# Three transformer layers on one core: one norm chain for both token tiles, and a reordered first and second layer

## The chip, the core and the metric

The kernel runs on one core of a Trainium2 chip. The metric is the device time of one execution in microseconds (us). The kernel before took 1570.29 us, the median of three runs (1568.15 to 1570.87).

## What is computed

256 tokens of width 1024 (two tiles of 128 tokens) pass through three layers, all in float32. Each layer normalises x by its root mean square, modulates it by vectors made from a condition c, mixes tokens, adds the result to x, normalises again and sends every token to two of its experts.

```python
def first_block(x, c, ...):                 # layers 0 and 1
    silu_c = jax.nn.silu(c)
    for i in range(DEPTH):
        mod = silu_c @ ada_w[i] + ada_b[i]
        sh1, sc1, g1, sh2, sc2, g2 = [m[:, None, :] for m in jnp.split(mod, 6, axis=-1)]
        h = rms_norm(x, norm_mix_g[i]) * (1.0 + sc1) + sh1
        y = diff_attention(h, ...) if i % N_MIXERS == 0 else chunked_attention(h, ...)
        x = x + g1 * y
        h = rms_norm(x, norm_ffn_g[i]) * (1.0 + sc2) + sh2
        x = x + g2 * grouped_moe(h, router_w, router_bias, moe_w_gate[i], moe_w_up[i], moe_w_down[i])
    return x

def rms_norm(x, g):
    y = xf * lax.rsqrt(jnp.mean(xf * xf, axis=-1, keepdims=True) + NORM_EPS)
    return (y * g.astype(jnp.float32)).astype(x.dtype)

def grouped_moe(h, router_w, ...):          # 16 experts in 4 groups: best group, top 2 inside it
    scores = jax.nn.sigmoid((t @ router_w).astype(jnp.float32))
    ...
    for e in range(N_EXPERTS):
        he = jax.nn.silu(t @ w_gate[e]) * (t @ w_up[e])
        out = out + gates[:, e:e + 1] * (he @ w_down[e])
```

Layer 2 is a hybrid: a small gated MLP over chunks, attention over the tokens and over 256 context tokens (`ctx`, normalised and modulated with vectors of their own), a gated scan in both directions, and then 32 experts in 4 groups of 8.

## The kernel before

**Stages.** The layers run one behind the other. Times of the profiled execution, from the start of the span: start to 55, layer 0's mixing to 176, its router 176 to 205, the gather of tokens 205 to 218, its experts 222 to 441; layer 1's mixing 455 to 600, router 602 to 633, gather 634 to 644, experts 646 to 893; layer 2's mixing 907 to 1087, experts 1104 to 1564.

**Weights.** Every weight tile of 1 MB is fetched by SyncE's queue (SP) into one of 17 buffers called `u`, in the order in which the program uses them; the normalised x takes one as well. An issue waits until the buffer that it gets is free. Dense weights are split into a rounded part and a remainder for exact float32 products: ScalarE casts 128x2048 elements (L185) and VectorE subtracts (L196). The products themselves are L265.

**Order.** Two strings, MIX_ORDER[0] and [1], list the steps of the layers 0 and 1 in program order, a letter a step; a scheduler then orders the instructions of each engine, starting from that. Letters that matter here: `0` the norm and its transposes; `J` the broadcast of a gate; `A` and `f` one tile of modulation products (`ada_tile`, L410); `5`-`8` scores and softmax of a pair of heads; `V` a projection of values; `W`-`Z` transposes and value products of a pair of heads (`a_trans` L636, `head1` L691 and L693); `9` one step of the context's preparation for layer 2; `M` the router of one token tile (transposes L499, logits L1385 to L1405); `U` the broadcast of the second gate (bias sum L417, L440 on TensorE); `E` the ranks of the tokens in their experts (L1524 to L1530); `L` the gather of the tokens (L1559); `!` the overflow loop (L1720, L1721), at which every engine waits for the others and SP's stream of weights stops; `u` one weight tile of the experts ahead.

**The norm.** `norm` (L450) calls `norm_tile` for each token tile: a square with row sums on ScalarE (L457), ten tiny VectorE operations for 1/rms (L283 to L299, a bit trick and three Newton steps), and the scaling on VectorE (L459). It is used where a layer begins and for the context; `trans_split` (L477) then transposes the result on TensorE, eight blocks a tile, and L514 (ScalarE) and L516 (VectorE) apply the modulation. The router calls `norm_tile` itself.

**The next layer's modulation.** `done(key)` computes the tiles of modulation products that are left and closes the sum (`ada_close`: copy out of PSUM, L417, the turn to columns L425). `layer` calls it for the next layer ahead of the experts (`body`). The experts go in pairs; `body` loads 12 weight tiles a pair, forms gate and up products (L1641), transposes (L1657), down products (L1670), and adds the weighted results to x (L1705, L1711), two at a time.

## Time and profile before

| | |
|---|---|
| median of three runs | 1570.29 us (1568.15 to 1570.87) |
| the profiled execution | 1569.43 us |
| its span in the profile | 1567.7 us |
| TensorE (PE) busy | 1434.1 us, 91% of the span |
| VectorE (DVE) busy | 630.1 us, 40% |
| ScalarE (ACT) busy | 405.4 us, 26% |
| GpSimd (POOL) busy | 111.7 us, 7% |
| transferred | 540.87 MB, mean 345 GB/s |

The profile is one execution on the chip. About 1.7 us of it lie around the span. Busy shares are means over stages with different limits, so they do not tell what a change in one stage is worth; the timeline of each engine in a stage, with what ended each wait, does. TensorE's granted clock (PEclk) has two levels: 1.00 stands for 2.4 GHz and 0.50 for 1.2 GHz.

### The profile page before, as it was taken

The numbers are of one execution on the slowest core, as the hardware profiler recorded it, in microseconds if no ns is written. First come the engines' busy times: TensorE is split into PE (matmuls) and PEld (weight loads), VectorE is DVE, ScalarE is ACT, GpSimd is POOL, SyncE is SP. The second block draws the span as 40 slices with busy tenths as digits, with TensorE's granted clock in tenths as the row PEclk, the third lists the DMA queues.
The fourth block names the chain that finished last, engine by engine and source line by source line (L and its number), as shares of the span: only waits on it lengthen the run. The fifth ranks groups of instructions, "written<-read, shape, count | busy, mean of one in ns | idle before, by whom it ended". The sixth has DMA issues, their size and how long they took to land. (4 is left out here: it accounts for less than half of the span.)

```text
span 1567.7 us, 18587 instructions
## 1 busy us (share of the span) xinstructions
PE 1434.1 (91%) x7202; PEld 763.8 (49%) x7202; DVE 630.1 (40%) x1434; ACT 405.4 (26%) x717; POOL 111.7 (7%) x96
## 2 busy tenths in 40 slices
PE   5999989999989989899999899688999999989987
PEld 1676643454346556444544375465445445434432
DVE  3777521221276675242221368966122212212112
ACT  2455211011053553142110256532111111011000
POOL 0000101101000001001000000101000101001000
PEclk8999879999999999999999999899999999999999
DMA  9987859999989948499999768238799999999997
GB/s 362 321 330 273 333 203 422 420 422 421 413 310 380 334 161 321 189 416 416 417 420 419 268 212 301 89 103 327 294 421 422 421 421 420 422 421 421 421 421 294
DMA packets 131072, 540.87 MB, mean 345 GB/s; under 512 B 8600, under 2 KB 13856, under 8 KB 83360
## 3 DMA queue, kind: packets, MB, share of 16 engines
q1 hardware_dynamic: 128032, 533.73, 85.9%
q10 hardware_dynamic: 2320, 3.89, 0.8%
q0 software_dynamic: 624, 1.98, 0.4%
q8 instruction: 60, 0.98, 0.3%
q14 instruction: 36, 0.29, 0.1%
HBM read 538.49 MB, written 1.06 MB: 344 GB/s over the span
## 5 line engine op out<-in xcount | busy, mean ns | idle before, releaser
L1641 PE MATMUL ps<-u,b 128*64 128x512 f32 x2048 | 486.2, 599 | 13.7 <-DMA u<-in_w_dram 9.7
L1641 PEld LDWEIGHTS ps<-u,b 128*64 128x64 f32 x2048 | 165.9, 138 | 302.0 <-issue 278.6
L265 PE MATMUL ps<-u 128*128 128x512 f32 x1104 | 278.6, 403 | 6.3 <-ACT u L514 5.1
L265 PEld LDWEIGHTS ps<-u 128*128 128x128 f32 x1104 | 203.7, 190 | 78.5 <-issue 21.6
L1670 PE MATMUL ps<-u,b 128*64 128x512 f32 x1024 | 232.5, 597 | 5.0 <-ACT b L1659 2.4
L1711 DVE TENSOR_TENSOR x<-x,ps 128x512 f32<-128x512 f32 x128 | 79.7, 682 | 209.6 <-PE ps L1705 209.6
L1670 PEld LDWEIGHTS ps<-u,b 128*64 128x64 f32 x1024 | 83.1, 136 | 126.2 <-issue 115.5
L1677 POOL TENSOR_TENSOR b<-b,b 128x512 fp32r<-128x512 f32 x58 | 78.1, 1362 | 808.9 <-ACT b L1676 713.1
L1675 DVE SCALAR_TENSOR_TENSOR b<-ps,tiny,G 128x512 f32<-128x512 f32 x64 | 48.1, 751 | 183.9 <-PE ps L1670 175.5
L1648 DVE TENSOR_TENSOR b<-b,ps 128x512 f32<-128x512 f32 x32 | 22.0, 688 | 224.5 <-PE ps L1641 132.3
L196 DVE TENSOR_TENSOR u<-u 128x2048 fp32r<-128x2048 f32 (+1 forms) x48 | 105.4, 2208 | 4.8 <-ACT u L185 4.6
L410 PE MATMUL ps<-u,z 128*32 128x512 f32 x576 | 85.4, 650 | 16.8 <-DVE z L379 13.1
L1676 ACT CAST b<-b 128x512 fp32r<-128x512 f32 x64 | 39.4, 618 | 208.7 <-DVE b L1675 208.7
L1659 ACT COPY b<-ps 128x512 f32<-128x512 f32 x32 | 18.8, 586 | 274.2 <-PE ps L1657 274.2
L185 ACT CAST u<-u 128x2048 fp32r<-128x2048 f32 x44 | 82.7, 1912 | 17.9 <-DMA u<-in_a_w_qkv_dram 15.3
L1559 PE MATMUL ps<-b,u 128*128 128x512 f32 x256 | 77.0, 447 | 3.1 <-DVE b L1545 3.1
L1559 PEld LDWEIGHTS ps<-b,u 128*128 128x128 f32 x256 | 66.7, 329 | 19.6 <-issue 13.5
L1705 PE MATMUL ps<-b,b 128*128 128x512 f32 x256 | 70.2, 410 | 3.3 <-DVE b L1677 1.9
L1646 ACT ACTIVATE b<-ps 128x512 f32<-128x512 f32 x32 | 19.1, 597 | 191.7 <-PE ps L1641 191.7
L1705 PEld LDWEIGHTS ps<-b,b 128*128 128x128 f32 x256 | 45.2, 188 | 41.8 <-ACT b L1646 16.2
L514 ACT ACTIVATE b<-ps,mod,mA 128x512 f32<-128x512 f32 x32 | 24.9, 779 | 109.4 <-PE ps L1559 109.4
L516 DVE TENSOR_SCALAR b<-ps,mA,mod 128x512 f32<-128x512 f32 x32 | 25.9, 810 | 66.3 <-PE ps L1559 66.3
(346 smaller groups left out, 1167.0 us busy)
## 6 DMA issues: line engine op xcount, KB each, us to landing
u<-in_w_dram SPq DMA_DIRECT2D x192, 1024.0 KB, 19.8
u<-in_moe_w_gate_dram SPq DMA_DIRECT2D x64, 1024.0 KB, 11.1
u<-in_moe_w_up_dram SPq DMA_DIRECT2D x64, 1024.0 KB, 12.6
u<-in_moe_w_down_dram SPq DMA_DIRECT2D x64, 1024.0 KB, 13.2
u<-in_ada_w_dram SPq DMA_DIRECT2D x48, 1024.0 KB, 10.3
u<-in_w_mod_dram SPq DMA_DIRECT2D x24, 1024.0 KB, 7.3
u<-in_w_in_dram SPq DMA_DIRECT2D x14, 1024.0 KB, 5.7
u<-in_a_w_qkv_dram SPq DMA_DIRECT2D x12, 1024.0 KB, 14.7
```

Source lines behind the costliest of these rows:

```text
L185: (e.copy if e is self.nc.scalar else e.tensor_copy)(out, in_)
L196: self.pick(site, options).tensor_tensor(out, a, b, op=op)
L265: self.nc.tensor.matmul(p, x[a][:, k, t * 128:(t + 1) * 128], w[b][:, k % 4], start=start and i == 0 and k == ks[0], stop=stop and i == 2 ...
L410: self.nc.tensor.matmul(st["R"][32 * j:32 * j + 32, :], z[:, k, 11 - i:43 - i], w[:, k, :], start=(n == 0 and k < 4), stop=(last and k >= ...
L1559: nc.tensor.matmul(p, q[:, t, k:D:KC], P[:, t], start=(t == 0 and i == 0), stop=(t == 1 and i == 1))
L1641: nc.tensor.matmul(p[s * 64:(s + 1) * 64, :], hs[k // 2][:, k % 2, c0 + s * 64:c0 + (s + 1) * 64], W[e0, nm, k // 4, s][:, k % 4, :], star ...
L1670: nc.tensor.matmul(po[n][s * 64:(s + 1) * 64, :], heT[:, k, s * 64:(s + 1) * 64], w(s), start=(k == 0), stop=(k == 3), skip_group_check=True)
L1675: V.scalar_tensor_tensor(o, po[n], gs, g2[:, n * 512:(n + 1) * 512], op0=OP.mult, op1=OP.mult)
L1676: A.copy(oh[:, n], o)
L1677: (G if more else V).tensor_tensor(ol[:, n], o, oh[:, n].bitcast(F32), op=OP.subtract)
L1705: ins = nc.tensor.matmul(p, PT[:, t * 128:(t + 1) * 128], o[:, n, :], start=(i == 0), stop=(i == len(ops) - 1))
L1711: nc.vector.tensor_add(xs, xs, p)
```

## The change

It has six parts.

- `norm` squares half rows: four ScalarE operations of 128x512, first the left halves of both tiles, then the right ones. The sums of both tiles go through **one** chain of operations on 128x2, which has 13 steps, since the shorter form of the Newton step needs a value of its own for each row. Tile 0 is scaled on VectorE and tile 1 on ScalarE.
- In the routers of the layers 0 and 1 a Sigmoid of a constant is computed after the second tile's copy; its result is not used.
- MIX_ORDER[0]: the last two `A` steps move from the stretch behind the gather to places around the ranks and the gate's broadcast. The closing of the next layer's modulation (`done`) moves from ahead of `body` to behind the down products of its first pair of experts.
- MIX_ORDER[1], softmax: the step `X` moves behind the first `8`.
- MIX_ORDER[1], router: `U` moves from between the two `M` to behind `E`, next to the ranks.
- `head1`: the products of two heads take turns, key tile by key tile, where one head came behind the other.

```diff
--- before.py
+++ after.py
@@ -121,8 +121,8 @@
 RAW = 2
 
...
-MIX_ORDER = ("00kkfkqiqvtfvqr4vf421321Kxw3xuzwzfKfyQKQyfVnTVQRAn55667JV78A8o.WPYXWXZYZfNpNeafbMdDuMEUFOLAuu,LuuuluuuuAu!uu",
-             "0A0kkkqqqtvfvviffrKA12324341fKQxfKwxfyyQzzfQAIwTVR557667VJ.XV88oPYWWXYZ9Z9peabMdDUM9EFOLuLluuuuuuuuu!uuuu")
+MIX_ORDER = ("00kkfkqiqvtfvqr4vf421321Kxw3xuzwzfKfyQKQyfVnTVQRAn55667JV78A8o.WPYXWXZYZfNpNeafbMdDuMAEAUFOLuu,Luuuluuuuu!uu",
+             "0A0kkkqqqtvfvviffrKA12324341fKQxfKwxfyyQzzfQAIwTVR557667VJ.V8X8oPYWWXYZ9Z9peabMdDM9EUFOLuLluuuuuuuuu!uuuu")
...
@@ -325,7 +325,7 @@
         self.identR = self.per("identR", [128, 128], F32R)
         V.tensor_copy(self.identR, early_t("ident"))
         self.ident = self.identR.bitcast(F32)
-        one = self.per("one", [128, 1])
+        one = self.one = self.per("one", [128, 1])
         G.memset(one, 1.0)
         self.ones = one.to_broadcast([128, 128])
         self.unit = self.per("unit", [128, 44])
@@ -449,8 +449,20 @@
 
     def norm(self, x):
 
+        V, A = self.nc.vector, self.nc.scalar
         xn = self.t("u", [128, NT, D])
-        return xn, [self.norm_tile(xn[:, t], x[:, t]) for t in range(NT)]
+
+        ss = self.t("tiny", [128, 2, NT])
+        for n in range(2):
+            for t in range(NT):
+                c = slice(n * 512, (n + 1) * 512)
+                A.activation(xn[:, t, c], x[:, t, c], AF.Square, accum_out=ss[:, n, t:t + 1])
+        v = self.t("tiny", [128, NT])
+        V.tensor_add(v, ss[:, 0], ss[:, 1])
+        r = self.rstd(v, NT, D)
+        V.tensor_scalar(xn[:, 0], x[:, 0], r[:, 0:1], None, op0=OP.mult)
+        A.activation(xn[:, 1], x[:, 1], AF.Copy, scale=r[:, 1:2])
+        return xn, r
 
     def norm_tile(self, xn, x):
         ss = self.t("tiny", [128, 1])
@@ -685,13 +697,12 @@
             yield
             v = vs[g]
             po = self.ps()
-            for m in range(2):
-                ov = po[m * 64:(m + 1) * 64]
-                vh = slice((2 * j + m) * 64, (2 * j + m + 1) * 64)
-                nc.tensor.matmul(ov[:, 0:256], v[:, 0, vh], aTs[m][:, 0:256], start=True, stop=False,
-                                 skip_group_check=True)
-                nc.tensor.matmul(ov[:, 128:256], v[:, 1, vh], aTs[m][:, 256:384], start=False, stop=True,
-                                 skip_group_check=True)
+
+            for kt, out, keys in ((0, slice(0, 256), slice(0, 256)), (1, slice(128, 256), slice(256, 384))):
+                for m in range(2):
+                    vh = slice((2 * j + m) * 64, (2 * j + m + 1) * 64)
+                    nc.tensor.matmul(po[m * 64:(m + 1) * 64, out], v[:, kt, vh], aTs[m][:, keys], start=(kt == 0),
+                                     stop=(kt == 1), skip_group_check=True)
             hi, lo = (q[:, 4 * g + j] for q in oT())
             self.copy("oh", hi, po[:, :256])
             V.tensor_tensor(lo, po[:, :256], hi.bitcast(F32), op=OP.subtract)
@@ -1508,6 +1519,9 @@
                 rs = self.norm_tile(xn, self.x[:, t])
                 rt(lg[:, t], xT, rs)
                 self.copy("xh", xh[:, t], xn)
+                if l < 2 and t:
+
+                    A.activation(self.t("tiny", [128, 1]), self.one, AF.Sigmoid)
                 self.tt("xl", xl[:, t], xn, xh[:, t].bitcast(F32), OP.subtract, "GV")
                 yield
 
@@ -1619,7 +1633,7 @@
 
         acts["!"] = lambda: self.overflow(l, E, st["xs"], A_, B_, gates, st["mask"], rk, ov, ni, st["g2"], wg, wu, wd)
 
-        def body():
+        def body(close):
             g2, nxt = st["g2"], st["nxt"]
             hs, P = st["hs"], st["Pt"]
             pend = []
@@ -1681,6 +1695,8 @@
                         for n in range(2):
                             for k in range(2 * h, 2 * h + 2):
                                 down(n, k, lambda s: W[e0, "d", h, s][:, k % 2, n * 512:(n + 1) * 512])
+                    if not pr_:
+                        close()
                     next(side, None)
                     for n in range(2):
                         weigh(n)
@@ -1826,9 +1842,7 @@
                 self.mix(l, stB, (steps, acts))
             else:
                 self.mix2(stB, (steps, acts))
-            if nxt:
-                done(f"A{l + 1}")
-            body()
+            body((lambda: done(f"A{l + 1}")) if nxt else (lambda: None))
 
         if 0 in L:
             ada(0, 0, 4, "A0")
```

VectorE between layer 0's experts and layer 1's projections: L196 of 128x2048 are weight splits, L459 (L463 after) the scaling of a token tile, the tiny operations the chain of 1/rms. Before:

```order
L290 SCALAR_TENSOR_TENSOR tiny<-tiny 128x1
L294 SCALAR_TENSOR_TENSOR tiny<-tiny 128x1
L196 TENSOR_TENSOR u<-u 128x2048
L459 TENSOR_SCALAR u<-x,tiny 128x1024
L196 TENSOR_TENSOR u<-u 128x2048
L516 TENSOR_SCALAR b_3092<-ps,tiny,mod_84 128x256
```

After (L528 is L516 of before):

```order
L292 TENSOR_TENSOR tiny<-tiny 128x2
L293 SCALAR_TENSOR_TENSOR tiny<-tiny 128x2
L196 TENSOR_TENSOR u<-u 128x2048
L294 SCALAR_TENSOR_TENSOR tiny<-tiny 128x2
L196 TENSOR_TENSOR u<-u 128x2048
L463 TENSOR_SCALAR u<-x,tiny 128x1024
L528 TENSOR_SCALAR b_3072<-ps,tiny,mod_84 128x256
```

Both splits now stand ahead of the first scaling, with the last step of the chain between them.

TensorE in layer 1's router: L410 are modulation products, L440 the gate's broadcast, L499 (L511 after) the transposes of the second tile, L521 (L533) products of the context, L1524 to L1528 (L1538 to L1542) the ranks, L1559 (L1573) the gather. Before:

```order
L410 MATMUL ps<-u,z_123 32x512 x8
L440 MATMUL ps<-b_4485,cst 128x512 x2
L499 MATMUL ps<-identR,x 128x128 x8
L1385 MATMUL ps<-b_4495,b_4039 32x128 x8
L1404 MATMUL ps<-cst,b_4542 128x16
L521 MATMUL ps<-u 128x512 x8
L940 MATMUL ps<-identR,b_4550 128x128 x4
L1524 MATMUL ps<-tiny,cst 128x16
L1525 MATMUL ps<-tiny,cst 128x16
L1526 MATMUL ps<-tiny,one 128x16
L1528 MATMUL ps<-tiny,one 128x16 x2
L1559 MATMUL ps<-b_4601,u 128x512 x32
```

After:

```order
L511 MATMUL ps<-identR,x 128x128 x8
L1396 MATMUL ps<-b_4442,b_4019 32x128 x8
L1415 MATMUL ps<-cst,b_4489 128x16
L533 MATMUL ps<-u 128x512 x8
L951 MATMUL ps<-identR,b_4499 128x128 x4
L1538 MATMUL ps<-tiny,cst 128x16
L1539 MATMUL ps<-tiny,cst 128x16
L1540 MATMUL ps<-tiny,one 128x16
L1542 MATMUL ps<-tiny,one 128x16 x2
L410 MATMUL ps<-u,z_112 32x512 x8
L440 MATMUL ps<-b_4562,cst 128x512 x2
L1573 MATMUL ps<-b_4572,u 128x512 x32
```

L410 and L440 moved from ahead of the second tile's transposes to between the ranks and the gather.

VectorE ahead of the turn to columns (L425) in layer 1, for which TensorE needs L417: L185 copies sums out of PSUM, L697 (no row of it after) takes the remainder of the values' result, L459 (L463) scales the context. Before:

```order
L294 SCALAR_TENSOR_TENSOR tiny<-tiny 128x1
L459 TENSOR_SCALAR u<-u,tiny 128x1024
L697 TENSOR_TENSOR u<-ps,u 128x256 x3
L185 COPY b_4212<-ps 128x512
L697 TENSOR_TENSOR u<-ps,u 128x256
L417 TENSOR_TENSOR b_4212<-b_4212,b_3463 32x512
```

After (L725 is L714 of before, a part of the output's sum):

```order
L292 TENSOR_TENSOR tiny<-tiny 128x2
L293 SCALAR_TENSOR_TENSOR tiny<-tiny 128x2
L294 SCALAR_TENSOR_TENSOR tiny<-tiny 128x2
L463 TENSOR_SCALAR u<-u,tiny 128x1024
L185 COPY b_4192<-ps 128x512
L725 TENSOR_TENSOR b_4333<-ps,b_4012 128x512
L417 TENSOR_TENSOR b_4192<-b_4192,b_3443 32x512
```

The context's chain, which stood ahead of the values' results, now stands between them and L417.

## Rows read from the trace of the kernel before

**Rows 1.** The page's chain of work that ended last: shares of the span by line

```profile
DMA u<-in_w_dram 12%; PE ps L1641 8%; PE ps L1670 4%; PE ps L1559 1%; PE ps L1705 1%; PE ps L1657 0%; DVE b L1648 0%; ACT b L1659 0%; DVE x L1711 0%; PE ps L1570 0%; DVE b L1675 0%; DVE b L1677 0%; DVEq L1880 0%; PE ps L1568 0%; SPq L1600 0%
```

**Rows 2.** Windows: stretch, engines' busy us (instructions), clock, DMA share, GB/s

```profile
250.00:300.00 50.00, 48.93 (x230) 19.96 (x228) 10.35 (x19) 5.41 (x10) 4.40 (x4) 1.00 1.01 421
...
1130.00:1300.00 170.00, 166.64 (x749) 74.51 (x746) 35.97 (x61) 20.52 (x36) 19.53 (x14) 1.00 1.01 421
```

**Rows 3.** Timeline, TensorE, layer 0 to 1: start, us, engine, line, operation, shapes, count, [wait]

```profile
446.57 1.94 PE L477 MATMUL ps<-identR,u 128*128 128x128 f32 x8 [4.35 <-DVE tiny L283]
...
451.14 1.16 PE L477 MATMUL ps<-identR,u 128*128 128x128 f32 x8 [1.08 <-DVE u L459]
452.23 1.06 PE L410 MATMUL ps<-u,z 128*32 128x512 f32 x8
...
454.39 1.89 PE L265 MATMUL ps<-u 128*128 128x512 f32 x7 [0.43 <-ACT u L514]
```

**Rows 4.** Timeline, VectorE, the same seam: chain's start, scaling, weight split

```profile
443.70 0.15 DVE L299 TENSOR_SCALAR tiny<-tiny 128x1 f32<-128x1 f32 x1 [0.62 <-ACT u L457]
...
445.67 0.75 DVE L459 TENSOR_SCALAR u<-x,tiny 128x1024 f32<-128x1024 f32 x1
...
448.13 2.29 DVE L196 TENSOR_TENSOR u<-u 128x2048 fp32r<-128x2048 f32 x1
```

**Rows 5.** Timeline, ScalarE, the same seam: two casts of weights

```profile
444.61 3.68 ACT L185 CAST u<-u 128x2048 fp32r<-128x2048 f32 x2
```

**Rows 6.** Windows of three stretches at half clock

```profile
442.78:449.61 6.83, 3.04 (x16) 1.77 (x16) 5.68 (x24) 5.51 (x6) 0.00 (x0) 0.50 1.05 386
565.66:572.49 6.83, 4.22 (x17) 2.83 (x18) 3.24 (x11) 2.85 (x12) 0.00 (x0) 0.50 0.31 116
...
896.75:906.99 10.24, 7.50 (x32) 3.54 (x32) 9.86 (x25) 6.76 (x11) 0.00 (x0) 0.50 0.32 108
```

**Rows 7.** Timeline, TensorE, layer 1 to 2: first transposes, first projections

```profile
898.83 1.94 PE L477 MATMUL ps<-identR,u 128*128 128x128 f32 x8 [4.36 <-DVE tiny L283]
...
907.06 3.24 PE L265 MATMUL ps<-u 128*128 128x512 f32 x13
```

**Rows 8.** Timeline, TensorE, layer 1: values, softmax transposes, turn to columns

```profile
523.63 0.66 PE L691 MATMUL ps<-b,b 128*64 128x256 f32 x4
...
568.27 1.63 PE L636 MATMUL ps<-identR,b 128*128 128x128 f32 x6 [5.38 <-DVE b L196]
...
579.85 0.65 PE L691 MATMUL ps<-b,b 128*64 128x256 f32 x2
...
589.32 2.10 PE L425 MATMUL ps<-cst,b 128*64 128x12 f32 x32
```

**Rows 9.** Timeline, VectorE, layer 1: the softmax's reciprocal

```profile
565.89 0.18 DVE L618 RECIPROCAL tiny<-tiny 128x4 f32<-128x4 f32 x1 [1.61 <-ACT b L616]
```

**Rows 10.** Timeline, TensorE, layer 1's router: broadcast, transposes, gather

```profile
615.99 2.97 PE L440 MATMUL ps<-b,cst 128*128 128x512 f32 x4 [2.67 <-DVE b L417]
618.75 1.78 PE L499 MATMUL ps<-identR,x 128*128 128x128 f32 x8
...
634.21 9.45 PE L1559 MATMUL ps<-b,u 128*128 128x512 f32 x32 [1.54 <-DVE b L1545]
```

**Rows 11.** Timeline, VectorE, layer 1's router: x complete, comparison behind the sigmoid

```profile
612.51 0.69 DVE L196 TENSOR_TENSOR x<-x,b 128x512 f32<-128x512 f32 x1
...
627.12 0.90 DVE L1415 TENSOR_TENSOR tiny<-tiny,cst 128x32 f32<-128x32 f32 x1 [2.51 <-ACT tiny L1413]
```

**Rows 12.** Timeline, GpSimd, layer 1's router: subtraction

```profile
625.62 2.35 POOL L196 TENSOR_TENSOR u<-b,u 128x1024 fp32r<-128x1024 f32 x1 [10.22 <-ACT u L185]
```

**Rows 13.** Timeline, ScalarE, layer 1's router: table load

```profile
625.56 1.28 ACT L1413 ACT_TABLE_LOAD   x1
```

**Rows 14.** Timeline, SP's queue, layer 0: first issues behind the overflow loop

```profile
218.96 10.17 SPq L1600 DMA_DIRECT2D u<-in_moe_w_gate_dram  x4
```

**Rows 15.** Timeline, TensorE, layer 0: the turn to columns ahead of the experts

```profile
220.65 2.11 PE L425 MATMUL ps<-cst,b 128*64 128x12 f32 x32 [2.37 <-DVE b L417]
```

## The prediction

> **What bounds the kernel now.** I read the chain of work that ended last first, then the windows, then TensorE's waits along the timeline, stage by stage. The chain ends in layer 2's mixture of experts: TensorE first, then weight transfers [rows 1]. The windows say the same. In layer 2's experts the 16 DMA engines are full (share 1.01) while TensorE still has 3.4 us free in 170 [rows 2]. A stage that only streams weights at full rate gives back nothing that happens ahead of it: whatever moves its start moves the end by as much. In layer 0's experts both are nearly full (48.93 of 50 us busy, DMA 1.01) [rows 2]. The time that is left to win or lose therefore lies in the seams between stages, where TensorE waits. The change touches five of these: the start of layer 0's experts, the two seams in which a layer begins, layer 1's softmax, and layer 1's router.
>
> **1. The seam between layers 0 and 1 (one chain for both tiles).** Before, tile 0's chain of ten tiny VectorE operations starts at 443.70, when its square on ScalarE ends, and runs to 445.67, about 0.20 us a step; its scaling (0.75) follows at once [rows 4]. TensorE starts tile 0's eight transposes at 446.57, then fills with modulation products (L410, 1.06 for eight rows at full clock), waits 1.08 for tile 1 and transposes it at 451.14, in 1.16 [rows 3]. Two weight splits (L196, 128x2048, 2.29 us) stand on VectorE, one before and one behind tile 1's scaling [rows 4].
> After, the squares take the halves of x as they come. Tile 1's last half is ready when tile 0's is and its square is one more short one: a cast of 2048 columns costs 1.84 [rows 5], so 512 columns cost at least 0.46, and I allow 0.65. Both sums are there at 443.4 to 444.0; I take 443.8. The chain now has 13 steps: 13 x 0.20 = 2.6, to 446.3. But the order shows what stands in it: **both** splits come ahead of the scaling of tile 0, one before the chain's last step and one behind it. Their inputs do not hold them back: the casts, 1.84 each, follow the squares and end about 445.7 and 447.5. So VectorE goes 446.3 + 2.29 + 0.2 + 2.29 = 451.0 and the scaling (0.75) ends at 451.75. Tile 1's scaling on ScalarE is done by then, but the first transposes take tile 0. TensorE begins 451.75 instead of 446.57, and both groups of L410 (1.1 us each at full clock) now stand behind all 16 transposes.
> What it costs: at full clock 16 transposes (2.2, since neighbours overlap) and the two groups (2.1) end at 456.0. At half clock all of it takes twice that, to 460. Before, the projections (L265) run from 454.39, behind a wait of 0.43 and with two of them (0.5) already done; that is an unbroken start at 453.9, and I use 454.2, since short waits follow [rows 3]. That gives +1.85 to +5.8. Rows decide the clock: it stood at 0.50 from 442.78 to 449.61, that is for 3.0 us after TensorE came back at 446.57 [rows 3, 6]. With the same 3.0 after 451.75 (1.5 us of work done in it, 2.8 left) the end is 457.55. I take **+3.3**.
>
> **2. The seam between layers 1 and 2.** It is the same program: transposes at 898.83 and projections at 907.06 [rows 7], 452.3 later than in the first seam. Tile 0's scaling then ends at 451.75 + 452.26 = 904.0. At full clock the projections start at 908.3, with 3.0 us at half clock at 909.8, all at half clock at 912. The clock was at half for longer here, to 906.99, 8.2 us after the first transpose [rows 6, 7], so before lost more here and after can lose less on top. +1.3 to +5; I take **+2.8**.
>
> **3. Start of layer 0's experts.** The same 24 rows of modulation products run, but the last 16 now stand inside the gather and no longer behind it, so the gather ends about 1.9 later; the closing product (L425) moves from ahead of the experts to behind their first pair. Before, TensorE waited 2.37 for VectorE ahead of 220.65 and spent 2.11 on L425 [rows 15]; the experts began at about 222.7. SP, whose stream stops at the overflow loop, restarted at 218.96 [rows 14]. After, the loop is passed about 1.1 later (SP at 220.1), and the experts begin there: 2.5 earlier. L425's 2.11 come back later, where TensorE has 1 us free in 50 and DMA is full. Transfers: the three free buffers are filled either way, and the fourth waits for TensorE, so the stream behind it moves up by nearly the 2.5. The stage ends -0.4 (TensorE sets it) to -2.5 (DMA sets it) earlier. **-1.5**. The other side: if TensorE no longer idles long enough here to have its clock lowered, another 2 to 3 us; the clock row is not known for that gap, and it is in the range only.
>
> **4. Layer 1's softmax, value products and the context norm.** Before, TensorE waits 5.38 for the normalised scores at 568.27 [rows 8]; VectorE had a weight split ahead of the first reciprocal, but that one still waited 1.61 for exponentials, until 565.89 [rows 9]. After, the remaining score products run first on TensorE and the split stands behind the first softmax, but the exponentials on ScalarE are no earlier: reciprocal 565.89, two multiplies of some 0.5 each, transposes at 566.65. That is 1.6 earlier, with 1.6 of score products already done, and it may save part of the 2.1 that half clock cost there (4.22 busy in a stretch at 0.50, work that full clock does in half the time) [rows 6]. The value products of two heads in turn overlap: four L691 took 0.66 where they stood in turn and two took 0.65 where they did not [rows 8], so some 0.4 a pair at three pairs, -1.1.
> That gain meets a new wait. The context norm was spread over VectorE's gaps and done before the values; its chain, now one of 13 steps, stands behind the value copies and **ahead** of the bias sum (L417) for which L425 waits. Values end about 581; four squares 2.4, chain 2.6, scaling 0.75, two copies and L417 about 2: L425 starts at 588 to 589.5, against 589.32 before [rows 8], with TensorE idle some 3 us ahead of it. From -1.2 (no low clock) to +3 (clock low for what follows). **+0.4**.
>
> **5. Layer 1's router ahead of the gate broadcast.** Before, TensorE waits 2.67 for L417, does the broadcast (L440, 2.97) and only at 618.75 transposes the router's second tile [rows 10], though x was complete at 613.20 (612.51 plus 0.69) [rows 11]. So the router's chain moves up by some 5.4, to the ranks at about 627. But L410 and L440 now stand between the ranks and the gather (L1559): 1.1 to 1.9 of L410, then L185 and L417 on VectorE behind the ranks' own operations (to about 631), then L440, 2.0 at full clock and 2.97 at half. The gather starts at 633.0 to 634.5, against 634.21 [rows 10], and loses less or more of its clock. -2.4 to +1.2. **-0.8**.
>
> **6. At nothing.** The dummy Sigmoid moves a table load (1.28 us) off the router's chain [rows 13]. In layer 1 the load ends at 626.84, but the small operation that needs the sigmoid takes 0.90, from 627.12 to 628.02 [rows 11], and ends with GpSimd's subtraction (625.62 to 627.97) [rows 12]: it is held by that and not by the load. Bounds -0.3 to +0.3. The Trainium skill, "ScalarE: Activation LUTs", section "What ACT_TABLE_LOAD costs", gives a switch 1.28 us of load and 1.38 of drain, 2.66 in all. By that the two routers would win 5.3 and the sum below would be -1. The load's own length agrees; of a drain the rows show nothing. At the kernel's start the norm hides under the wait for modulation weights: 0, with 0.5 either way.
>
> **The sum.** 3.3 + 2.8 - 1.5 + 0.4 - 0.8 = +4.2. The profiled execution took 1569.43 (span 1567.7 and 1.7 around it), which gives 1573.6; the median of the three runs lies 0.86 above that execution, so the time to expect is 1574.5, 0.27% slower.
>
> **Rivals.**
> - Not slower, because the stalls are won outright: the softmax gains its 1.6 + 1.1 and the 2.1 of clock and the context norm hides behind fills (-4.8), the router -2.4, layer 0's experts -2.5, the seams at full clock +1.85 + 1.3. Sum -6.6: 1563.7. It decides if TensorE waits under 1 us at L425 in layer 1 and at the gather. For it: the two longest waits in layer 1 are these. Against it: in the new order both rows on which TensorE then waits stand behind longer queues. 0.20.
> - The same: the seams at full clock and the rest as summed, +0.4: 1570.7; or the seams as forecast and one of the stalls won. 0.25.
> - The table loads count. By the rows' 1.28 each, twice, the sum is +1.6: 1571.9. 0.05.
> - Slower by more: both seams at half clock throughout (+5.8, +5) and the context wait with low clock (+3), the rest as summed, +11.5: 1581.8. 0.15.
>
> **How the numbers follow.** The forecast has 0.35. A measurement of this kernel tells 0.2%, 3.1 us, from no change. Of the forecast's cases most lie above 1573.4, some below. Faster 0.20, same 0.31, slower 0.49. The range drops the far ends of the first and the last rival: 1566 to 1580.
>
> **What would show it.** Right: in both seams VectorE does two 128x2048 splits before the scaling of tile 0, and TensorE's wait for the first transpose grows from 4.4 to 9 or 10 us; a wait of 3 us at L425 in layer 1 near 588; at the router a wait at L440 and not at the second tile's transposes; experts of layer 0 from about 220. Layer 2's experts keep their length. Wrong: if the splits are not held to that place or the clock stays full, the seams cost half; if L425 does not wait, point 4 is a gain of 4; if the end of layer 0's experts does not move, point 3 is nothing.

## The result, and the profile after

The changed kernel took 1581.61 us (median of 4 runs, 1581.16 to 1581.97) against 1570.36 us of the kernel before beside it: a ratio of 1.0074, with a 95% interval of 1.0058 to 1.0090. It is slower by 11.3 us. The prediction had the direction and the seams, but not the size: 1574.5 was forecast, and 1581.6 lies outside its range of 1566 to 1580. The span of the profiled execution grew by 12.4 us, from 1567.7 to 1580.1. TensorE's line of the page hardly changed:

```profile
PE 1438.1 (91%) x7202; PEld 764.9 (48%) x7202; DVE 624.6 (40%) x1402; ACT 412.5 (26%) x739; POOL 112.0 (7%) x96
```

Where the 12.4 us are is told by windows that begin and end with a stage. Both tables give the stretch, its length, each engine's busy time with the number of its instructions (PEld is TensorE's loading of weights), the mean granted clock, the DMA share and GB/s. Line by line: layer 0's experts, the seam to layer 1, layer 1's mixing with router and gather, its experts, the seam to layer 2, layer 2's mixing with router and gather. Of the kernel before:

```profile
core 0: us, PE busy (x) PEld busy (x) DVE busy (x) ACT busy (x) POOL busy (x), PEclk, DMA share, GB/s
222.59:442.22 219.63, 211.82 (x942) 91.22 (x940) 44.42 (x77) 24.96 (x43) 18.70 (x14) 0.99 1.01 414
442.22:453.23 11.01, 5.58 (x34) 2.90 (x33) 9.86 (x28) 7.34 (x10) 0.00 (x0) 0.69 1.05 383
453.23:646.10 192.87, 178.29 (x998) 120.00 (x994) 123.42 (x301) 85.45 (x170) 9.55 (x8) 0.96 0.72 262
646.10:894.47 248.37, 238.74 (x1050) 107.03 (x1050) 63.17 (x134) 46.05 (x74) 20.30 (x17) 1.00 0.99 400
894.47:907.06 12.59, 7.57 (x33) 3.55 (x33) 11.48 (x31) 8.81 (x13) 0.00 (x0) 0.59 0.32 109
907.06:1104.88 197.82, 169.21 (x1182) 120.67 (x1178) 145.97 (x360) 91.68 (x153) 11.58 (x11) 0.93 0.55 199
```

Of the changed kernel:

```profile
220.32:442.55 222.23, 214.37 (x970) 92.94 (x970) 45.87 (x79) 27.37 (x48) 18.71 (x14) 0.99 1.01 415
442.55:457.61 15.06, 5.64 (x33) 3.72 (x33) 11.32 (x26) 9.99 (x15) 0.00 (x0) 0.66 0.83 298
457.61:649.72 192.11, 178.10 (x999) 120.95 (x995) 119.93 (x287) 85.03 (x172) 9.80 (x8) 0.96 0.72 259
649.72:899.79 250.07, 240.47 (x1050) 107.43 (x1050) 63.18 (x134) 47.35 (x78) 20.29 (x17) 0.99 0.98 398
899.79:914.87 15.08, 5.77 (x33) 3.72 (x33) 11.75 (x27) 9.48 (x14) 0.00 (x0) 0.66 0.24 82
914.87:1117.29 202.42, 171.94 (x1182) 121.18 (x1178) 143.16 (x356) 91.43 (x153) 11.61 (x11) 0.92 0.54 195
```

| stage | before | after | difference | forecast |
|---|---|---|---|---|
| start to layer 0's ranks | 200.27 | 199.18 | -1.1 | 0 |
| ranks to experts, layer 0 | 22.33 | 21.13 | -1.2 | -1.5 with the next line |
| experts of layer 0 | 219.63 | 222.23 | +2.6 | |
| seam 0 to 1 | 11.01 | 15.06 | +4.05 | +3.3 |
| layer 1: mixing, router, gather | 192.87 | 192.11 | -0.8 | -0.4 (points 4 and 5) |
| experts of layer 1 | 248.37 | 250.07 | +1.7 | 0 |
| seam 1 to 2 | 12.59 | 15.08 | +2.5 | +2.8 |
| layer 2: mixing, router, gather | 197.82 | 202.42 | +4.6 | 0 |
| experts of layer 2 | 458.78 | 458.79 | 0.0 | 0 |

The two seams cost 6.5 us, where 6.1 were forecast. Layer 1's experts and layer 2's mixing, in which TensorE does the same instructions in the same order as before, cost another 6.3, and layer 0's gather and experts cost 1.4 where they were to give 1.5. The first line isn't read: between kernels that change nothing there it lay between 198.1 and 200.8.

**The seams.** VectorE in the seam from layer 0 to layer 1, timeline of the changed kernel (start, duration, engine, line, operation, operands; in brackets the idle time ahead and what ended it). L461 begins the common chain, L294 is its last step, L196 are the weight splits, L463 scales tile 0. It answers to [rows 4]:

```profile
444.21 0.16 DVE L461 TENSOR_TENSOR tiny<-tiny 128x2 f32<-128x2 f32 x1 [0.80 <-ACT u L459]
...
446.60 2.29 DVE L196 TENSOR_TENSOR u<-u 128x2048 fp32r<-128x2048 f32 x1
448.81 0.15 DVE L294 SCALAR_TENSOR_TENSOR tiny<-tiny 128x2 f32<-128x2 f32 x1
448.88 2.28 DVE L196 TENSOR_TENSOR u<-u 128x2048 fp32r<-128x2048 f32 x1
451.08 0.75 DVE L463 TENSOR_SCALAR u<-x,tiny 128x1024 f32<-128x1024 f32 x1
```

Tile 0 is scaled at 451.83; the forecast was 451.75. TensorE waits for it, does both tiles' transposes (L489) at once, then two groups of L410, then the projections. The same in both seams, for [rows 3, 7]:

```profile
451.97 3.65 PE L489 MATMUL ps<-identR,u 128*128 128x128 f32 x16 [9.42 <-DVE u L463]
455.55 2.13 PE L410 MATMUL ps<-u,z 128*32 128x512 f32 x16
...
909.10 3.65 PE L489 MATMUL ps<-identR,u 128*128 128x128 f32 x16 [9.32 <-DVE u L463]
912.68 2.26 PE L410 MATMUL ps<-u,z 128*32 128x512 f32 x16
914.87 1.43 PE L265 MATMUL ps<-u 128*128 128x512 f32 x5
```

Waits of 9 to 10 us were forecast, and the projections of layer 1 at 457.55; they began at 457.61. The transposes ran at half clock (3.65 for sixteen), the 16 L410 nearly all at full clock (2.13).

**Layer 0's experts.** They begin 2.3 us earlier (2.5 was forecast), but L425 (1.98) now lies in a stage that has no room, and the weighted adds (L1721) of the second pair are spread in it. TensorE of the changed kernel:

```profile
220.32 2.69 PE L1655 MATMUL ps<-u,b 128*64 128x512 f32 x6 [1.98 <-DVEq L1737]
...
245.19 1.98 PE L425 MATMUL ps<-cst,b 128*64 128x12 f32 x32
...
278.94 1.19 PE L1721 MATMUL ps<-b,b 128*128 128x512 f32 x4
280.07 3.65 PE L1655 MATMUL ps<-u,b 128*64 128x512 f32 x14
283.64 0.73 PE L1721 MATMUL ps<-b,b 128*128 128x512 f32 x2
284.31 1.07 PE L1655 MATMUL ps<-u,b 128*64 128x512 f32 x2
285.31 0.73 PE L1721 MATMUL ps<-b,b 128*128 128x512 f32 x2
```

Before, eight adds (L1705 there) stood together in 2.11:

```profile
280.13 2.11 PE L1705 MATMUL ps<-b,b 128*128 128x512 f32 x8
```

Now they stand as 4, 2 and 2 in 2.65, among products of another shape (L1655, 64 rows wide).

**Layer 1.** It begins 4.4 us later than before. TensorE's waits stand where the forecast had them: 2.61 for the softmax (at 570.44), 3.17 at L425 and, in the router, 1.87 at L440.

```profile
591.90 2.11 PE L425 MATMUL ps<-cst,b 128*64 128x12 f32 x32 [3.17 <-DVE b L417]
...
621.93 9.47 PE L533 MATMUL ps<-u 128*128 128x512 f32 x16
...
632.57 0.29 PE L1538 MATMUL ps<-tiny,cst 128*128 128x16 f32 x2
...
637.48 1.98 PE L440 MATMUL ps<-b,cst 128*128 128x512 f32 x4 [1.87 <-DVE b L417]
638.90 8.37 PE L1573 MATMUL ps<-b,u 128*128 128x512 f32 x32
```

The ranks (L1538) came at 632.57, which is 628.2 on the clock of before; 627 was forecast. The context's products (L533) stand ahead of them in TensorE's queue, and a good part of these ran at half clock (mean 0.75). Layer 1's experts then begin in a stretch at half clock, in which the kernel before had none:

```profile
650.58:654.00 3.42, 3.42 (x10) 0.97 (x8) 0.00 (x0) 0.23 (x1) 0.00 (x0) 0.50 0.87 304
```

### The profile page after: what moved, and what is told of

It is laid out like the page before. It is cut to its first block, busy times and chain, and to the rows that moved or that the text cites. A ratio compares the mean times of both kernels' runs of the same rounds, so it can differ in the third digit from the quotient of the medians.

```text
span 1580.1 us, 18571 instructions
## 1 busy us (share of the span) xinstructions
PE 1438.1 (91%) x7202; PEld 764.9 (48%) x7202; DVE 624.6 (40%) x1402; ACT 412.5 (26%) x739; POOL 112.0 (7%) x96
## 3 DMA queue, kind: packets, MB, share of 16 engines
q0 software_dynamic: 624, 1.98, 0.4%
## 5 line engine op out<-in xcount | busy, mean ns | idle before, releaser
L1655 PE MATMUL ps<-u,b 128*64 128x512 f32 x2048 | 488.5, 600 | 15.6 <-DMA u<-in_w_dram 9.7
L1655 PEld LDWEIGHTS ps<-u,b 128*64 128x64 f32 x2048 | 166.2, 138 | 304.2 <-issue 280.8
L196 DVE TENSOR_TENSOR u<-u 128x2048 fp32r<-128x2048 f32 (+1 forms) x48 | 105.2, 2207 | 5.1 <-ACT u L185 4.9
L410 PE MATMUL ps<-u,z 128*32 128x512 f32 x576 | 83.8, 648 | 17.3 <-DVE z L379 13.2
L185 ACT CAST u<-u 128x2048 fp32r<-128x2048 f32 x44 | 82.5, 1910 | 17.9 <-DMA u<-in_a_w_qkv_dram 15.3
L1573 PE MATMUL ps<-b,u 128*128 128x512 f32 x256 | 75.7, 440 | 1.6 <-DVE b L1559 1.6
L1573 PEld LDWEIGHTS ps<-b,u 128*128 128x128 f32 x256 | 66.0, 328 | 19.2 <-issue 15.5
L1721 PE MATMUL ps<-b,b 128*128 128x512 f32 x256 | 70.8, 411 | 3.3 <-DVE b L1691 1.9
L1721 PEld LDWEIGHTS ps<-b,b 128*128 128x128 f32 x256 | 45.0, 188 | 43.3 <-ACT b L1660 16.2
L528 DVE TENSOR_SCALAR b<-ps,mA,mod 128x512 f32<-128x512 f32 x32 | 25.9, 810 | 71.1 <-PE ps L1573 71.1
## 6 DMA issues: line engine op xcount, KB each, us to landing
u<-in_moe_w_gate_dram SPq DMA_DIRECT2D x64, 1024.0 KB, 12.2
```

Source lines behind the costliest of these rows:

```text
L185: (e.copy if e is self.nc.scalar else e.tensor_copy)(out, in_)
L196: self.pick(site, options).tensor_tensor(out, a, b, op=op)
L410: self.nc.tensor.matmul(st["R"][32 * j:32 * j + 32, :], z[:, k, 11 - i:43 - i], w[:, k, :], start=(n == 0 and k < 4), stop=(last and k >= ...
L1573: nc.tensor.matmul(p, q[:, t, k:D:KC], P[:, t], start=(t == 0 and i == 0), stop=(t == 1 and i == 1))
L1655: nc.tensor.matmul(p[s * 64:(s + 1) * 64, :], hs[k // 2][:, k % 2, c0 + s * 64:c0 + (s + 1) * 64], W[e0, nm, k // 4, s][:, k % 4, :], star ...
L1721: ins = nc.tensor.matmul(p, PT[:, t * 128:(t + 1) * 128], o[:, n, :], start=(i == 0), stop=(i == len(ops) - 1))
```

## The experiments

Four questions were open: are the splits the cost of the seams; is the rest chance; which part of the change brings the rest; and can a stage that nobody touched become longer because the work ahead of it is shifted? "Shift" below means that some products of layer 1's fourth pair of experts are done once or twice more, and the last result replaces the others.

### The seams: what gets in between the chain and its user

**e1_old_norm** is the changed kernel with the norm of before; **e2_norm_only** is the kernel before with the new norm alone. The edit of e2, which e1 takes back:

```diff
     def norm(self, x):
         xn = self.t("u", [128, NT, D])
-        return xn, [self.norm_tile(xn[:, t], x[:, t]) for t in range(NT)]
+        ss = self.t("tiny", [128, 2, NT])
...
+        r = self.rstd(v, NT, D)
+        V.tensor_scalar(xn[:, 0], x[:, 0], r[:, 0:1], None, op0=OP.mult)
+        A.activation(xn[:, 1], x[:, 1], AF.Copy, scale=r[:, 1:2])
+        return xn, r
```

**e3_pinned** is the changed kernel with the first two weight splits of layers 1 and 2 held in program order, that is behind the scaling; **e4_before_pinned** does the same to the kernel before.

```diff
-        def split():
+        def split(pin=False):
...
-            self.tt("sv", lo, w, hi.bitcast(F32), OP.subtract, "V")
+            ins = self.nc.vector.tensor_tensor(lo, w, hi.bitcast(F32), op=OP.subtract)
+            if pin:
+                self.tc.keep_in_program_order(ins)
...
             for _ in range(PRIME):
-                w.split()
+                w.split(l == 1)
...
-                w.split()
+                w.split(True)
```

Expected of e1:

> The changed kernel with the norm of before (a chain for each tile), the other parts kept. Theory A (the norm costs only what the two seams show, about 5.5 us, and the clock that falls in other places later follows from when stages begin): near 1576, with 3 us either way for the clock; TensorE's wait for the first transpose of each seam falls from 9.4 to 4.4. Rival B (the norm is behind all of it, layer 1's experts and layer 2's mixing included): 1570. Layer 0's experts still lose what they gain at their start, since that is not the norm's.

Of e2:

> The kernel before with the new norm alone. Theory A: +5.5 us in the seams, near 1576, 3 either way. Rival B (the norm is behind all): 1582. Rival C (the seams give their loss back later): 1570.

Of e3:

> The changed kernel with one thing more: the first two weight splits of layers 1 and 2 are held behind the scaling of tile 0 on VectorE. Theory A (the splits' place costs the time, not the single chain): the scaling ends about 4.5 us earlier in each seam, TensorE's wait falls from 9.4 to 4.9, the projections begin near 453.3 in the seam between layers 0 and 1 instead of 457.6, and the time falls by 8 to 9 us to 1573, 3 either way. Rival (the longer chain and the scaling on ScalarE cost it): falls by less than 3 us.

Of e4:

> The kernel before with the first two weight splits of layers 1 and 2 held behind the scaling of both tiles. Theory A: tile 1 is scaled 2.2 us earlier in each seam, but the splits end 0.1 later; the projections begin 1 to 1.5 us earlier a seam: 1567 to 1569. Rival (the splits end the wait for the projections, so nothing is won): 1570.

Measured: e1 1575.25 (1.0033, 1.0020 to 1.0046), e2 1581.63 (1.0079, 1.0062 to 1.0095), e3 1575.36 (1.0035, 1.0021 to 1.0049), e4 1571.94 (1.0014, 1.0004 to 1.0023). VectorE, then TensorE, in the first seam of e3:

```profile
447.95 0.75 DVE L465 TENSOR_SCALAR u<-x,tiny 128x1024 f32<-128x1024 f32 x1
448.62 4.65 DVE L247 TENSOR_TENSOR u<-u 128x2048 fp32r<-128x2048 f32 x2
```

```profile
448.85 3.65 PE L491 MATMUL ps<-identR,u 128*128 128x128 f32 x16 [5.13 <-DVE u L465]
452.43 2.67 PE L412 MATMUL ps<-u,z 128*32 128x512 f32 x16
455.03 4.16 PE L267 MATMUL ps<-u 128*128 128x512 f32 x17
```

With both splits behind the scaling TensorE's wait falls from 9.42 to 5.13, and the seams last 11.31 and 11.32 instead of 15.06 and 15.08. So the splits' place, and not the common chain, is the seams' cost: this is shown. (The common chain alone leaves the one wait of 5.13, where the kernel before has two, of 4.35 and 1.08.) With the old norm and all else of the change (e1) the seams last 12.68 and 12.60, so that there the new norm costs 2.4 and 2.5; alone (e2) it costs 4.6 and 2.1. The 1.7 by which e1's first seam is longer than before is half clock, which cost TensorE 3.8 there and 1.5 before. By its median e3 is 6.2 faster than the changed kernel, where 8 to 9 were expected, by its profiled run 5.4, where 7.5 left the seams: 1.2 went to the first layer's start, whose length differs from kernel to kernel, and 0.8 to the mixing of layers 1 and 2. e4 missed: its seams are 0.2 and 1.1 shorter than before, but layer 2's mixing, router and gather, whose instructions are the same, took 201.60 instead of 197.82, and the kernel became slower. And the norm alone (e2) costs 12.2 while all else without it (e1) costs 5.9: the parts do not add up to 11.3. e1 came out near its theory A. e2 has the number of its rival B, which e1 refutes: without the new norm layer 1's experts (250.22) and layer 2's mixing (201.10) stayed long. Of e2's 12.6 in the profile the seams are 6.7.

### Chance, or the same each time

e5 is the kernel before once more, and e6 the changed one; neither has an edit.

> The kernel before, unchanged, profiled once more. It measures how far layer 2's mixing and its gather (197.8 us of TensorE's time from the first projection to the experts in the first profile of before, 202.4 in that of the changed kernel, with the same order of instructions) vary from one execution to the next. Theory P (the difference is where TensorE's half clock happens to fall): this execution gives a value anywhere from 197 to 203. Theory Q (the change sets it): 197 to 198.5 again.

> The changed kernel, unchanged, profiled once more. Theory P: layer 2's mixing and gather take anything from 197 to 203, layer 1's experts 248.4 to 250.1. Theory Q: 202 to 203 again, and layer 1's experts 250.0 again. The seams' idle times, 9.4 and 9.3, come back in either.

e5 took 1570.22 and e6 1582.10. Layer 2's mixing, router and gather lasted 197.85 and 202.52 (first profiles: 197.82 and 202.42), layer 1's experts 248.29 and 249.87 (248.37 and 250.07). So far as two executions each can tell, the longer stages belong to the kernel, not to the execution. Other runs of the kernel before lay anywhere from 1567.4 to 1573.9, and none at the ends of that range was profiled.

### The other parts

**e7_layer0_parts**: the kernel before with the new MIX_ORDER[0] and the closing moved into `body`. **e8_close_soft_val**: before with that closing, the later `X` and the value products in turn. **e11_router_order_only**: before with `U` behind `E` and nothing else. **e12_without_norm_and_tiles**: the changed kernel without the new norm and the new MIX_ORDER[0]. **e16_after_keep_adds**: the changed kernel with the weighted adds of layer 0's second pair kept together.

e7, and without its first two lines a part of e8:

```diff
-MIX_ORDER = ("...dDuMEUFOLAuu,LuuuluuuuAu!uu",
+MIX_ORDER = ("...dDuMAEAUFOLuu,Luuuluuuuu!uu",
...
-            if nxt:
-                done(f"A{l + 1}")
-            body()
+            body((lambda: done(f"A{l + 1}")) if nxt else (lambda: None))
```

e11, then e16:

```diff
-...9Z9peabMdDUM9EFOLuLluuuuuuuuu!uuuu")
+...9Z9peabMdDM9EUFOLuLluuuuuuuuu!uuuu")
```

```diff
-                    self.scatter(pend, range(2))
+                    self.scatter(pend, range(2), keep=l == 0 and pr_ == 2)
...
-                    if len(ns) == 1:
+                    if keep or len(ns) == 1:
                         self.tc.keep_in_program_order(ins)
```

e12 takes these parts of the change back, and keeps the rest:

```diff
-MIX_ORDER = ("...dDuMAEAUFOLuu,Luuuluuuuu!uu",
+MIX_ORDER = ("...dDuMEUFOLAuu,LuuuluuuuAu!uu",
...
-        r = self.rstd(v, NT, D)
...
+        return xn, [self.norm_tile(xn[:, t], x[:, t]) for t in range(NT)]
```

> The kernel before with the two parts in layer 0 alone: the two late tiles of modulation products moved ahead, the closing behind the first pair of experts. Theory A (what the experts win at their start, 2.3 us, the closing and an extra spreading of the weighted adds take back, 1.9 and 1.5): the stretch from the ranks to the end of the experts is 1.0 to 1.8 us longer, the time 1570.5 to 1573. Rival (the prediction's step: the experts end 1.5 earlier): 1568.

> The kernel before with three parts alone: the closing behind the first pair (without the two moved tiles), the later softmax transposes, the value products in turn. In this order of instructions the weighted adds of the second pair of experts stay together. Theory A (the adds' spreading comes from the two moved tiles): layer 0's experts begin 2 us earlier and end 0.3 to 1 earlier. Softmax and values: TensorE idles 2.7 less and works 1.1 less, and the context norm stays where it was: 1 to 4 us less in layer 1's mixing. Time 1565.5 to 1568.5. Rival (both parts meet waits further on, as in the whole change): 1569 to 1571.

> The kernel before with the gate's broadcast behind the ranks in layer 1, nothing else. By the prediction's step 5 the gather starts between 1.2 earlier and 0.3 later and the experts between 2.4 earlier and 1.2 later. Theory A (the work moves from one side of the ranks to the other; 1 to 1.5 us are won before the clock, and what the clock makes of it depends on when the experts begin): from the first projection of layer 1 to the experts 190 to 192.5 against 192.9; the time 1567 to 1573, layer 1's experts 248.3 or 250.

> The changed kernel without the new norm and without the two moved tiles of modulation products in layer 0. Theory A: layer 0's stretch from ranks to the end of the experts 2.5 us shorter than in the changed kernel, both seams 2 to 4 shorter, layer 1's mixing and router as there. Leaving the clock aside 1566 to 1568; with what it takes in layer 1's experts and layer 2 1566 to 1574.

> The changed kernel with the weighted adds of layer 0's second pair of experts held together on TensorE behind the next pair's products. Theory A (their spreading among 64-row products costs 1 to 1.5 us): layer 0's experts 220.7 to 221.3 us instead of 222.2; what that does to the total hangs on the clock behind it. Rival (the order of the adds costs nothing): 222.2.

| | time | ratio (95%) | what its stages showed |
|---|---|---|---|
| e7 | 1570.60 | 1.0004 (0.9994 to 1.0014) | layer 0: ranks to experts 20.97, experts 222.24 |
| e8 | 1571.89 | 1.0016 (1.0007 to 1.0025) | 20.13 and 219.59; L425 of layer 1 waits 3.61 |
| e11 | 1569.96 | 1.0011 (1.0001 to 1.0021) | layer 1's mixing to gather 190.99, its experts 249.85, layer 2's mixing 200.88 |
| e12 | 1571.45 | 1.0019 (1.0008 to 1.0031) | 20.19 and 219.90; 191.35; 250.34; 200.95 |
| e16 | 1580.39 | 1.0069 (1.0055 to 1.0084) | layer 0's experts 220.98 |

- Layer 0: with the closing moved and the two tiles where they were (e8) the way from the ranks to the experts is 2.2 shorter and the experts keep their length. That isn't because L425 is free in there: half clock cost these experts 2.6 before and nothing in e8. With the moved tiles (e7) they take 2.6 more, since half clock is back (1.71) and the weighted adds are spread. Kept together (e16), these make the stage 1.26 shorter, as expected; the same adds on TensorE as in the rows above:

```profile
269.78 13.90 PE L1655 MATMUL ps<-u,b 128*64 128x512 f32 x64
283.61 2.12 PE L1721 MATMUL ps<-b,b 128*128 128x512 f32 x8
```

- The first seam takes back what layer 0 won: in every kernel with the closing moved and the old norm (e1, e7, e8, e12, e14) it lasts 12.7 instead of 11.0, with half clock at a cost of 3.8 instead of 1.5. With 1.4 more in layer 1's experts, and 0.3 less in layer 1's mixing where 1 to 4 were expected, e8's time missed its forecast of 1565.5 to 1568.5.
- Layer 1's context norm: I expected it to keep its early place in e8, which has the old norm. It did not; L425 waited 3.61 there, longer than in the changed kernel. The late place comes from the moved softmax and values, not from the chain of both tiles.
- The router: `U` alone wins 1.9 where it was put (e11), and the run is no faster: 1.5 go in layer 1's experts and 3.1 in layer 2's mixing. No instruction of either was touched. (The first layer's start is 2.2 shorter in its profile, with nothing changed in it, so the sum of its stages is +0.5.)

### A shift alone

The kernel before with a shift in layer 1's experts: **e9_shift1** repeats two products (TensorE's row of L1641 there lasts 8.75 us instead of 7.89), **e10_shift2** repeats them twice, four more in all (9.60). Nothing else differs, and layer 2's instructions are those of before, in the same order.

```diff
-                        for s in range(2):
+                        for s in [0, 1] * (1 + (1 if l == 1 and pr_ == 3 and nm == "g" and k == 0 else 0)):
```

**e13_router_order_shift** is e11, **e14_without_two_shift** e12 with one product repeated. That was to cost 0.47 us, but the row grew from 7.89 to 8.75 in both, as with the two products of e9. **e15_after_shift** is the changed kernel with the four of e10.

```diff
-                        for s in range(2):
+                        for s in ((0, 0, 1) if l == 1 and pr_ == 3 and nm == "g" and k == 0 else range(2)):
```

> The kernel before with two matmuls repeated once in layer 1's fourth pair of experts (64x512 each, both with start set, so nothing else changes): all that follows begins 0.95 us later, in the same order of instructions. Theory S (the length of layer 2's mixing and gather is set by where their start falls among the steps of TensorE's granted clock): the two together change from 197.8 to between 201 and 203, the time rises by 4 to 6 us. Rival (their length in the changed kernel came from the norm's other instructions): the time rises by 0.95.

> The same with both matmuls repeated twice: everything behind begins 1.9 us later. Theory S: layer 2's mixing and gather take another length again, between 199 and 202 (as in the kernel with the norm alone, whose start fell about there), the time rises by 3 to 6 us. Rival: it rises by 1.9.

> The router's order alone (as in the run before) with one matmul of layer 1's fourth pair repeated once: all behind it begins 0.47 us later, so that layer 2's mixing would start where it starts in the kernel before among the clock's steps. Theory S: mixing and gather 197.8 again instead of 200.9, the time falls by 2.5 to 1567.5, below the kernel before. Rival (their length is not a matter of where they start): the time rises by 0.5 to 1570.5.

> The changed kernel without the new norm and without the two moved tiles, with the same 0.47 us later start. Theory S: layer 2's mixing and gather 197.8 instead of 201.0, 1568 to 1569.5. Rival: 1571.9.

> The changed kernel, whole, with both matmuls repeated twice: layer 2 begins 1.9 us later. Theory S: its mixing and gather take 197.8 to 199.5 instead of 202.4 though the norm is the new one; the time 1579 to 1581 in spite of the later start. Rival (the new norm makes the mixing longer): 202.4 again, 1583.5.

Measured: e9 1570.71 (1.0004, 0.9994 to 1.0014; its profiled run, 1573.01, is the longest of ten), e10 1574.66 (1.0035, 1.0021 to 1.0050), e13 1568.62 (0.9998, 0.9989 to 1.0007), e14 1572.11 (1.0017, 1.0007 to 1.0026), e15 1582.95 (1.0085, 1.0071 to 1.0100). Layer 2's mixing, router and gather in the windows of e9 and of e10, columns as above:

```profile
906.91:1108.20 201.29, 171.58 (x1183) 120.38 (x1179) 147.53 (x364) 93.07 (x156) 11.58 (x11) 0.92 0.56 199
```

```profile
906.82:1110.44 203.62, 173.00 (x1183) 121.17 (x1179) 146.85 (x364) 93.10 (x156) 11.59 (x11) 0.92 0.55 196
```

The stage took 197.82 before, 201.29 in e9 and 203.62 in e10. It did not begin later: the seam ahead of it, with the same instructions, lasted 12.6 in the kernel before and 10.9 in e9 and e10, so that the projections begin at 907.06, 906.91 and 906.82, and in e9 and e10 TensorE waits again (0.43 and 0.44) behind the first two of them. Seam and stage together took 210.4, 212.2 and 214.5: 1.8 and 4.1 more.

In e10 and in the changed kernel a part of the difference can be pointed at. Some 60 us into the stage TensorE does eight L410 after a wait of 0.98 for ScalarE. Those eight in the kernel before, in e10 and in the changed kernel:

```profile
967.12 1.06 PE L410 MATMUL ps<-u,z 128*32 128x512 f32 x8
```

```profile
968.10 1.93 PE L410 MATMUL ps<-u,z 128*32 128x512 f32 x8
```

```profile
975.48 1.94 PE L410 MATMUL ps<-u,z 128*32 128x512 f32 x8
```

They run at half clock in the last two. In these the low stretches of the stage begin 60 us into it (61 in e10), and stand at 77, 94, 118 and 183 (about a us later in e10); in the kernel before the first is at 89, and in e9 at 90. Over the stage half clock cost TensorE 11.1 us before, 14.3 in e10 and 14.0 after (half of its busy time at 0.50), and its idle time was 28.6, 30.6 and 30.5. What is left, its work at full clock, is 158.1, 158.7 and 158.0. So the 4.6 us of the changed kernel are half clock and idle time, and no added work. Its waits are those of e10, on the same lines and within 0.3 us each, but for the 0.44 at e10's start, and none above 0.2 us is ended by a transfer.

So a shift ahead of the stage, with no instruction of the stage changed, alters where in it the clock falls, and with that its length. The time at which the stage begins does not tell where: e9 and e10 begin it within 0.1 us of each other, and those eight L410 run at half clock in e10 and at full clock in e9 (1.07 us). The whole times bear this out in part. e10's median is 5.2 above the kernel before (theory S: 3 to 6; the rival: 1.9), though its stage lies outside the 199 to 202 that was expected. e9's median is 1.3 above, and its interval holds no change at all; that fits the rival's 0.95 and not theory S's 4 to 6; its 201.29 comes from the longest of its ten runs.

A second sign is e13, which has 0.86 of work more than e11 and the lower ratio (0.9998 against 1.0011, though the intervals overlap): its layer 2's mixing took 199.04 instead of 200.88, its second seam 10.90 instead of 12.57. But which start is a good one could not be foretold: e14 was to bring the stage to 197.8 and it took 200.03, with the rival's time, and e15 was expected at 1579 to 1581 and took 1582.95, with 1.0 less in layer 2's mixing for 1.6 more in layer 1's experts. Since the one product cost 0.86, e13 and e14 did not reach the start that they were meant to test.

## Why the prediction was wrong, and where it was right

Two steps failed. The larger: the sum took every stage between the five seams at its old length, and two of these stages took 6.3 us more. The smaller: point 3's end of layer 0's experts, 2.9 us off. The rest was right within 0.8 us.

- **Points 1 and 2, right.** +6.1 was forecast and 6.5 measured (4.05 and 2.49). The order gave the cause, two splits ahead of the scaling, and e3 shows it by removing it. The clock was taken rightly in kind: half for the transposes, full for nearly all of L410. That the first seam's end came within 0.1 us (457.55 forecast, 457.61 measured) is luck in part: half clock lasted 4.05 us after TensorE came back, where 3.0 was taken, and the work was 3.6 us at full clock, where 4.3 was taken. The forecast also counts from an unbroken start at 454.2, the table from the first projection at 453.23; by the forecast's count the first seam lost 3.4 and layer 1's mixing, router and gather 0.2.
- **Point 3, wrong in sign: -1.5 was forecast and 1.4 lost.** The start was right (220.1 forecast, 220.32 measured). The step that failed is the stage's end, "-0.4 to -2.5". It had L425's 2.11 come back where 1 us in 50 is free, and still let the transfers carry most of the gain through. Measured, TensorE set the end: its idle time in the stage stayed (7.8 and 7.9), and its work grew by some 3.4: 2.6 of length, and 0.9 that half clock cost less. L425 is 2.0 of it and the spread of the weighted adds 1.26 (e16); the order showed the spread, and the prediction had not priced it. The "other side" that it kept for the range, the clock, is real: e8 won 2.6 by it, the changed kernel 0.9.
- **Points 4 and 5, right within 0.6** (-0.4 forecast, -0.76 measured by the table, +0.2 by the forecast's count), with details off that cancel. At L425 TensorE was 1.8 ahead of the kernel before, and lost that to half clock behind it (sixteen transposes, L511, in 3.67 instead of 2.05). The ranks waited for L533 in TensorE's queue and came 1.2 later than forecast, but the broadcast and the gather followed at full clock. The bias sum's wait at L425 was forecast as 3 and measured as 3.17; its cause was not the longer chain (e8). Two sums are off: point 4's reciprocal and two multiplies end at 567.1 and not at 566.65 (566.06 was measured, on the clock of before), and the rival "the same" with its seams at full clock and the rest as summed comes to +1.25 and not to +0.4.
- **Point 6, right as far as the trace shows; no run has the Sigmoid alone.** The table load moved ahead (620.40 to 621.68, the Sigmoid at 621.70), and VectorE's small operation still ended with GpSimd's subtraction, as in [rows 11, 12]. By the 2.66 us a switch of the Trainium skill, "ScalarE: Activation LUTs", "What ACT_TABLE_LOAD costs", the two routers would have won an estimated 5.3. The trace shows nothing of it. VectorE and GpSimd of the changed kernel:

```profile
624.23 2.31 DVE L1426 TENSOR_TENSOR tiny<-tiny,cst 128x32 f32<-128x32 f32 x1 [1.10 <-ACT tiny L1424]
626.57 0.18 DVE L1430 TENSOR_TENSOR tiny<-tiny 128x24 f32<-128x24 f32 x1
```

```profile
624.14 2.35 POOL L196 TENSOR_TENSOR u<-b,u 128x1024 fp32r<-128x1024 f32 x1 [4.32 <-ACT u L185]
```

- **The step that failed most: the stages in between, 6.3 us.** The prediction said that the time to win or lose lies in the seams, and added the five seams to stages of their old length. That holds for layer 2's experts (458.78 and 458.79) and for no other stage. Layer 1's experts lost 1.7, all of it one low stretch of the clock at their start, and layer 2's mixing 4.6. e10 shows that a shift alone can do this to layer 2's mixing. e1, e2, e8 and e11, four different edits, all lost 1.4 to 1.9 in layer 1's experts. All twelve profiles in which something in layer 1's mixing or router differs from before have that low stretch, and the six without such a difference (the kernel before, e4, e5, e7, e9, e10) have none. The start time does not decide it: e3 and e4 begin these experts at 647.68 and 647.69, and e3 alone has it.
- **The rival "slower by more" (1581.8) has the number and not the mechanism.** It wanted both seams at half clock throughout; their projections began where the forecast, and not the rival, had them.

What stays open: whether the changed kernel could have a start at which layer 2's mixing takes 198 again. The shift that tried it (e15) brought 201.4. That its 4.6 come from where the clock falls, and not from the different buffers that its scheduler gave out, is argued from e10's equal pattern and waits, not shown on the changed kernel itself. Why the clock falls where it does in one kernel and not in another stays open too.

No kernel beat the one before by more than its interval; e13, at 0.9998, came nearest.

## What to carry to other kernels

When a short chain is merged or shortened, read in the order what now stands between its last step and its user: two cheap splits that filled a gap before cost 4.3 us of waiting at each of two places. A stage in which one engine is nearly full does not absorb what is moved into it, and the same eight products cost more when they are spread among products of another shape. And where a stage has many short waits, its length is no constant: a shift of 1 to 2 us ahead of it changed it, counted with the seam before it, by 2 to 4 us one way or the other (e9, e10, e13), so a sum of edits needs that as an uncertainty of its own, and an edit is judged by the whole time beside its own stage.

## What the runs showed of the hardware

- With some 0.9 and 1.7 us of work added in the stage ahead, and its own instructions unchanged, a stage of 198 us became 3.5 and 5.8 us longer, and the seam ahead of it 1.7 shorter (e9, in its longest run; e10). The kernel before and the changed kernel each repeated that stage within 0.1 us in a second profile (e5, e6).
- TensorE's granted clock was 0.50 from 650.58 to 654.00, just behind the start of layer 1's experts and while it was fully busy, in the changed kernel; the kernel before had no half clock in that whole stage.
- A 128x32 operation on VectorE took 2.31 us beside a subtraction of 2.35 on GpSimd, and its neighbour of 128x24, behind it, 0.18.
